# Modulation batches placed directly behind the next group of small matmuls, instead of by a clock of their own

## The chip, the core and the metric

The kernel runs on one core of a Trainium2 chip. The metric is the device time of one execution in microseconds; for the kernel before it is 1811.66 us, the median of three runs (1810.25 to 1814.02). The engines are named as in the profile: PE (TensorE, matmuls), PEld (its weight loads), DVE (VectorE), ACT (ScalarE), POOL (GpSimd) and SP (SyncE, which here issues most DMAs). SP, like every engine, runs its instructions strictly in its own order.

## The reference, cut to what matters

One layer of a hybrid diffusion backbone is computed for 128 context tokens and 256 latent tokens, D = 2048, all in float32. The adaLN modulation is one product of a vector per token kind with a wide matrix:

```python
m = jax.nn.silu(cond) @ w + b          # cond (n, 2048), w (2048, 6 * 2048)
sh1, sc1, g1, sh2, sc2, g2 = jnp.split(m[:, None, :], 6, axis=-1)
hcur = x * (1 + sc1) + sh1             # then h @ w_in: attention, conv module, SSD scan
x = layer_norm(ALPHA * x + g1 * mix)   # mix = concat(three mixers) @ w_out
hcur = x * (1 + sc2) + sh2             # then the ConvFFN, gated by g2
```

Two of its six parts matter here: g1 (the gate of the first residual) and sc2 (the scale ahead of the ConvFFN). They are needed only after w_out, so their products can be done at any time before.

## The kernel before, in words

**The main stream.** Each large float32 product is done as three fp32r products (high parts and low parts of both operands), on PE, back to back, with whole 128x128 weights. They are recorded at L454 to L456 (tokens on the output partitions) and L460 to L462 (channels on the output partitions); this text calls each such instruction a *main*. Weights come from HBM in 512 KB pieces: SP issues the load into one of four `raw` buffers (L216), ACT copies it into a high part (L229), DVE subtracts for the low part (L230).

**The small work.** Between the mains, while the w_in columns of z/dt, v, k and q and the first column group of w_out are computed, PE also does everything that is small and float32: transposes of tokens (L418, L424), cumulative sums of dt (L498 to L503), states and chunk products of the scan (L541, L579, L584, L592, L608), LayerNorm sums (L372, L385), and attention: scores (L698, L701, L703), transposes of the probabilities (L726) and values (L739). They share two PSUM buffers (`at`); a group that needs a third waits until ACT or DVE has copied the first out.

**The modulation batches.** For g1 and sc2, 64 pieces of 512 KB (`wm`) are read. One piece gives four small matmuls with 32 output partitions and 256 columns (L786, each two PE instructions, so a batch of three pieces shows as x24). The pieces come in batches of three, into the three `v` buffers, so the loads of the next batch can be issued only as the matmuls of this one free the buffers. There are 22 batches, the 11th and 22nd of two pieces. After the 11th, `mod2_end(0)` adds the bias (L800, DVE) in a `v` buffer and writes the rows of g1 to HBM (L803, POOL); the third piece of batch 12 takes that buffer. After the 22nd, `mod2_end(1)` turns sc2 (L805, L809, L811).

**What sets the order.** On PE, the order in this stretch is the order in which the program is written out. `_Flow` keeps a planner's clock: `tick(us)` advances it with each group of mains, and a heap holds generators with the time at which each may go on. A generator yields (cost, delay): the cost advances the clock, and after the delay it may place its next group. The generators are `tok_gen`, `dt_gen`, `ssm_gen`, `conv_ln_gen`, `attn_gen`, `sh2_gen` and `mod2_gen(3, 12.0)`, whose 12.0 is the delay between the loads of a batch and its matmuls. `run` is called at most every 1.5 us of that clock. The other engines' queues are ordered by a scheduler that is not changed, from the same program.

Of the kernel before, what the change touches and what calls it, by code (L numbers as in the profile page):

```python
# [47 lines left out]
class _Flow:  # L48
# [2 lines left out]

    def __init__(self, step):
        self.now, self.last, self.n, self.q, self.bg, self.credit, self.step = 0.0, 0.0, 0, [], [], 0.0, step
        self.rate = 0.0

    def add(self, delay, gen):
        self.n += 1
# [2 lines left out]
    def run(self):  # L60
        self.last = self.now
        while self.q and self.q[0][0] <= self.now:
            gen = heappop(self.q)[2]
            said = next(gen, None)
            if said is not None:
                self.now += said[0]
                self.add(said[1], gen)

    def tick(self, us):
        self.now += us  # L70
# [12 lines left out]
    def drain(self):  # L83
        while self.bg:
            self.bg.pop(0)[0]()
        while self.q:
            self.advance()


# [10 lines left out]
def _build(tc, ctx, a):  # L100
# [16 lines left out]
    flow = _Flow(1.5)  # L117
# [232 lines left out]
    def conv31_steps(i):  # L350
        def first():
            do_glu(i)
            cvo[i] = t_t(399)
            V.tensor_scalar(out=cvo[i][:, :399], in0=glu[i][:, 0:399], scalar1=P_("conv_w", 31 * i),
                            scalar2=P_("conv_b", i), op0=ALU.mult, op1=ALU.add)

        def tap(j):
            V.scalar_tensor_tensor(out=cvo[i][:, :399], in0=glu[i][:, j:j + 399], scalar=P_("conv_w", 31 * i + j),
                                   in1=cvo[i][:, :399], op0=ALU.mult, op1=ALU.add)

        return [(first, 1.2)] + [(lambda j=j: tap(j), 0.63) for j in range(1, 31)]
# [46 lines left out]
    def do_conv5(i):  # L408
        o = t_t(386)
        taps(o, xbc_raw[i], lambda j: ("sconv_w", 5 * i + j), 5, P_("sconv_b", i), 386)  # L410
        S.activation(out=o, in_=o, func=AF.Silu)
        xact[i] = o

    def tok_gen():
        for c in range(3):
            ps = at_t()
            for i in range(4):
                PE.transpose(ps[:, 128 * i:128 * i + 128], xact[i][:, OFF[c]:OFF[c] + 128], ident)  # L418
            xtok[c] = m_t()
            S.copy(out=xtok[c], in_=ps)  # L420
            yield 0.5, 1.5
            ps = at_t()
            for i in range(2):
                PE.transpose(ps[:, 128 * i:128 * i + 128], xact[4 + i][:, OFF[c]:OFF[c] + 128], ident)  # L424
            btok[c] = sbt([128, 256], "btok", 3)
            S.copy(out=btok[c], in_=ps[:, :256])
            yield 0.3, 1.5
        ready.add("tok")
# [187 lines left out]
    def ssm_gen():  # L616
        while not {"tok", "dt"} <= ready:
            yield 0.0, 1.0
        yield from state_steps(0, 0)
        yield from state_steps(0, 1)  # L620
        yield from chunk_steps(0)
        load_state()
        yield from state_steps(1, 0)
        yield from state_steps(2, 1)
        yield from chunk_steps(1)
        yield from chunk_steps(2)
        ready.add("ssm")
        ready.update(range(12, 16))
# [147 lines left out]
    def mod2_start(g):  # L776
        gS[g] = gm_t()

    def mod2_load(i):
        g, half, k = i // 32, i // 16 % 2, i % 16  # L780
        return load(a["wm2"][g, half, k], 1024, v_t().rearrange("p a b -> p (a b)"))

    def mod2_piece(i, raw):
        g, half, k = i // 32, i // 16 % 2, i % 16
        for j in range(4):
            PE.matmul(gS[g][32 * j:32 * j + 32, 256 * half:256 * half + 256], cond[:, k, :],  # L786
                      raw[:, 256 * j:256 * j + 256], start=k == 0, stop=k == KC - 1)
# [5 lines left out]
    def mod2_end(g):  # L793
        ps = gS.pop(g)
        vv = v_t()
        sm, bg = vv[:, 0, :], vv[:, 1, :]
        if g == 0:
            pinned(bg, a["bgate"])
            with tc.high_priority(offset=HP):
                V.tensor_tensor(out=sm, in0=ps, in1=bg, op=ALU.add)  # L800
            gd[g] = dr.tile([2, D], F32, tag=f"gd{g}", name=nm("gd"))
            for j in range(4):
                G.dma_start(out=gd[g][:, 512 * j:512 * j + 512], in_=sm[32 * j:32 * j + 2, :])  # L803
            return
        V.tensor_copy(out=sm, in_=ps)  # L805
        yield 0.0, 2.0
        pt = at_t()
        for b in range(4):
            PE.transpose(pt[:, 128 * b:128 * b + 128], sm[:, 128 * b:128 * b + 128], ident)  # L809
        pv = pt.rearrange("p (b j c) -> p j b c", b=4, j=4)[:, :, :, 0:2]  # L810
        V.tensor_tensor(out=s2.rearrange("p (j b) c -> p j b c", j=4), in0=pv,  # L811
                        in1=bc(b2p.rearrange("p (j b) -> p j b", j=4), 3, 2), op=ALU.add)
        yield 0.5, 1.0

    def mod2_gen(most, gap):
        i = 0
        while i < 64:
            n = min(most, 32 - i % 32)
            raws = [mod2_load(j) for j in range(i, i + n)]
            yield 0.0, gap  # L820
            if i % 32 == 0:
                mod2_start(i // 32)
            for j, raw in enumerate(raws):
                mod2_piece(i + j, raw)
            i += n
            yield 0.45 + 0.43 * n, 0.0
            if i % 32 == 0:
                yield from mod2_end((i - 1) // 32)
# [52 lines left out]
    def sh2_gen(gap):  # L881
        while "ssm" not in ready:
            yield 0.0, 1.0
        for _ in range(3):
            sh2_load()
            yield 0.0, gap
        while "stop" not in ready:
            sh2_step()
            yield 0.0, gap
# [103 lines left out]
    with tc.manual_schedule(engines={mybir.EngineType.PE}):  # L993
        for i in range(8):
            do_conv5(i)
        for i in range(4):
            flow.bg += conv31_steps(i)
        flow.rate = 0.45
        flow.add(30.0, tok_gen())
        flow.add(0.0, mod2_gen(3, 12.0))  # L1000
        flow.add(40.0, conv_ln_gen())
        flow.add(30.0, ssm_gen())
        flow.add(50.0, attn_gen())
        flow.add(60.0, sh2_gen(4.0))
        phase_zd()
        flow.add(0.0, dt_gen())
        phase_v()
        flow.rate = 0.7
        for hp in range(8):
            k = qk_tile(0, hp)  # L1010
            qk[hp] = (qk_tile(1, hp), k)
        ps = [mm_t() for _ in range(3)]
        for k in ORDER[:12]:
            cat_split(k)
        wo_group(0, ps, cat_split, lambda last: flow.tick(2.09))
        ready.add("stop")
        flow.drain()
        gb = mix_rows(0)
        for t in range(3):
            mix_evac(t, 0, 0, 512, ps[t], gb)  # L1020
# [333 lines left out]
```

## Time and profile before

| what | value |
|---|---|
| median of three runs | 1811.66 us (1810.25 to 1814.02) |
| the profiled execution's own time | 1812.03 us |
| its span, first to last instruction | 1810.2 us |
| PE busy | 1780.8 us, 98% of the span |
| DVE busy | 1213.4 us, 67% |
| ACT busy | 774.6 us, 43% |
| modulation batches L786, first and last start | 240.4 us, 571.6 us |
| granted TensorE clock, mean | 0.998 |

The table says how long each engine had work. A PE that is busy 98% of the time leaves little room, but "busy" counts the pipelined length of a matmul, so a start-to-start distance is the better measure of what one costs. Idle time of PE is listed with what ended it.

### The profile page before, as it was taken

The page shows a single profiled execution, that of the slowest core. Times are in us where ns is not written, and L with a number is a line of the kernel's source. Part 1 is how long each engine was busy: PE and PEld are TensorE (multiplying, and loading weights), DVE is VectorE, ACT ScalarE, POOL GpSimd, SP SyncE. Part 2 cuts the span into 40 slices and gives each one's busy share as a digit, 9 for nine tenths or more (in the row PEclk, how much of TensorE's full clock was granted, in tenths as well). Part 3 has the DMA queues.
Part 4 walks back from the last instruction along what each step waited for, and adds up shares of the span by engine and source line. Part 5 has one row for each costly group of instructions (what it writes and reads, how often), then busy time and mean ns, then how long its engine had stood idle before and what let it go on. Part 6 is the DMA issues. An engine that isn't in the chain of part 4 may idle for free. (4 is left out here: it accounts for less than half of the span.)

```text
span 1810.2 us, 28844 instructions
## 1 busy us (share of the span) xinstructions
PE 1780.8 (98%) x10794; PEld 1620.9 (90%) x10794; DVE 1213.4 (67%) x2591; ACT 774.6 (43%) x1466; POOL 62.6 (3%) x149
## 2 busy tenths in 40 slices
PE   7999999999999999999999999999999999999998
PEld 6888997888887899999889999989999988999987
DVE  3866899885999566667535667535676544766577
ACT  4222454656764246444433444323444323444434
POOL 0000001110001000000000000000000000000000
PEclk9999999999999999999999999999999999999999
DMA  8999457766999452445444454444544544444454
GB/s 317 310 322 321 148 199 254 241 210 204 356 344 336 138 162 86 142 140 161 130 129 152 151 175 162 135 128 134 175 163 145 158 123 140 163 146 153 121 152 139
DMA packets 113259, 337.75 MB, mean 187 GB/s; under 512 B 13096, under 2 KB 17672, under 8 KB 113120
## 3 DMA queue, kind: packets, MB, share of 16 engines
q1 hardware_dynamic: 105888, 311.65, 52.2%
q0 software_dynamic: 7232, 24.28, 4.5%
q8 instruction: 84, 1.38, 0.3%
q14 instruction: 55, 0.45, 0.1%
HBM read 331.08 MB, written 4.79 MB: 186 GB/s over the span
## 5 line engine op out<-in xcount | busy, mean ns | idle before, releaser
L229 ACT CAST whi<-raw 128x512 fp32r<-128x512 f32 (+1 forms) x755 | 467.5, 620 | 869.1 <-PE mm L461 291.4
L230 DVE TENSOR_TENSOR wlo<-raw,whi 128x512 fp32r<-128x512 f32 (+1 forms) x755 | 519.8, 689 | 428.3 <-ACT whi L229 426.4
L460 PE MATMUL mm<-hl,whi 128*128 128x384 f32 x1245 | 425.2, 342 | 1.4 <-ACT whi L229 1.1
L461 PE MATMUL mm<-hl,whi 128*128 128x384 f32 x1245 | 419.5, 337 | 0.0
L462 PE MATMUL mm<-hl,wlo 128*128 128x384 f32 x1245 | 418.8, 336 | 0.0
L460 PEld LDWEIGHTS mm<-hl,whi 128*128 128x128 f32 x1245 | 233.6, 188 | 12.2 <-issue 5.5
L461 PEld LDWEIGHTS mm<-hl,whi 128*128 128x128 f32 x1245 | 233.8, 188 | 0.6 <-DVE wlo L230 0.2
L462 PEld LDWEIGHTS mm<-hl,wlo 128*128 128x128 f32 x1245 | 233.7, 188 | 0.0
L460 PE MATMUL sc<-hl,whi 128*128 128x384 f32 x659 | 222.8, 338 | 0.0
L461 PE MATMUL sc<-hl,whi 128*128 128x384 f32 x659 | 221.8, 337 | 0.0
L462 PE MATMUL sc<-hl,wlo 128*128 128x384 f32 x659 | 221.7, 336 | 0.0
L460 PEld LDWEIGHTS sc<-hl,whi 128*128 128x128 f32 x659 | 123.6, 188 | 2.9 <-ACT whi L229 1.6
L461 PEld LDWEIGHTS sc<-hl,whi 128*128 128x128 f32 x659 | 123.7, 188 | 0.1
L462 PEld LDWEIGHTS sc<-hl,wlo 128*128 128x128 f32 x659 | 123.7, 188 | 0.0
L843 DVE SCALAR_TENSOR_TENSOR junk<-raw,gb 128x512 bf16<-128x512 f32 x128 | 87.6, 684 | 51.1 <-DMA raw<-wg 50.9
L454 PE MATMUL mm<-whi,hl 128*128 128x512 f32 (+2 forms) x293 | 101.2, 345 | 0.1
L456 PE MATMUL mm<-whi,hl 128*128 128x512 f32 (+2 forms) x293 | 99.4, 339 | 0.0
L455 PE MATMUL mm<-wlo,hl 128*128 128x512 f32 (+2 forms) x293 | 99.3, 339 | 0.0
L456 PE MATMUL mm<-whi,t 128*128 128x512 f32 (+1 forms) x232 | 89.6, 386 | 0.0
L454 PE MATMUL mm<-whi,t 128*128 128x512 f32 (+1 forms) x232 | 89.6, 386 | 0.0
L843 DVE SCALAR_TENSOR_TENSOR junk<-m,m 128x512 bf16<-128x512 f32 x128 | 87.9, 687 | 2.5 <-DMA m<-wsh 0.6
L455 PE MATMUL mm<-wlo,t 128*128 128x512 f32 (+1 forms) x232 | 89.5, 386 | 0.0
(353 smaller groups left out, 2474.8 us busy)
## 6 DMA issues: line engine op xcount, KB each, us to landing
raw<-wu SPq DMA_DIRECT2D x176, 512.0 KB, 3.5
raw<-wd SPq DMA_DIRECT2D x79, 512.0 KB, 3.6
m<-wm SPq DMA_DIRECT2D x128, 256.0 KB, 5.7
v<-wm SPq DMA_DIRECT2D x64, 512.0 KB, 6.4
raw<-wA SPq DMA_DIRECT2D x32, 512.0 KB, 5.4
raw<-wqk SPq DMA_DIRECT2D x32, 512.0 KB, 4.5
m<-wsh SPq DMA_DIRECT2D x64, 256.0 KB, 6.1
raw<-wo SPq DMA_DIRECT2D x32, 512.0 KB, 4.7
```

The source lines that it names most:

```text
L229: S.copy(out=hi[:, :w], in_=rw)
L230: V.tensor_tensor(out=lo[:, :w], in0=rw, in1=hi[:, :w].bitcast(F32), op=ALU.subtract)
L454: PE.matmul(ps[:, :n], A, hi[:, w0:w0 + n], start=k == 0, stop=False)
L455: PE.matmul(ps[:, :n], A, lo[:, w0:w0 + n], start=False, stop=False)
L456: PE.matmul(ps[:, :n], B, hi[:, w0:w0 + n], start=False, stop=k == last)
L460: PE.matmul(ps[:, :T], A, hh[k], start=k == k0, stop=False)
L461: PE.matmul(ps[:, :T], A, hl[k], start=False, stop=False)
L462: PE.matmul(ps[:, :T], B, hh[k], start=False, stop=k == k1)
L843: V.scalar_tensor_tensor(out=j, in0=w, scalar=1.0, in1=cbc[s], op0=ALU.mult, op1=ALU.mult, accum_out=macc[:, 16 * s + kt, kq:kq + 1])
```

## The change

`mod2_gen` yields a delay of None after its loads have been there for the gap, which is now 4.0 instead of 12.0. The planner takes such a generator out of the heap and keeps it in `behind`; as soon as any generator has placed a group with a cost, all generators in `behind` are put at the front of the heap, so that a batch comes directly after that group. `drain` lets those that still wait go on at the end.

```diff
+        self.rate, self.behind = 0.0, []
...
             if said is not None:
                 self.now += said[0]
-                self.add(said[1], gen)
+                if said[1] is None:
+                    self.behind.append(gen)
+                else:
+                    self.add(said[1], gen)
+                if said[0] > 0:
+                    for other in self.behind:
+                        self.add(-1.0, other)
+                    self.behind = []
...
             raws = [mod2_load(j) for j in range(i, i + n)]
             yield 0.0, gap
+            yield 0.0, None
...
-        flow.add(0.0, mod2_gen(3, 12.0))
+        flow.add(0.0, mod2_gen(3, 4.0))
```

The lines added stand above the code, so a line number of the changed kernel is higher by 9 (or 10, below `mod2_gen`): its L795 is L786 here, L735 is L726, L707 is L698, L508 is L499.

**PE, 1926 mains into the main stream, in the attention of a pair of heads.** `gm` is the PSUM of the modulation, `v` a modulation piece; `at`, `p` and `sc` belong to attention. Before, batch 16 stands alone between mains:

```order
L462 MATMUL mm_5483<-hl_80,wlo_5487 128x384
L786 MATMUL gm_4726<-v_5344,cond_63 32x256 x4
L786 MATMUL gm_4726<-v_5346,cond_63 32x256 x4
L786 MATMUL gm_4726<-v_5348,cond_63 32x256 x4
L460 MATMUL mm_5483<-hl_80,whi_5486 128x384
```

At the same place of the main stream now batch 21 stands behind the transposes and scores:

```order
L471 MATMUL mm_5573<-hl_80,wlo_5577 128x384
L735 MATMUL at_5594<-cons_66,p_5481 128x128 x3
L735 MATMUL at_5600<-cons_66,p_5488 128x128 x3
L707 MATMUL sc_5606<-qk_5429,qk_5571 128x128
L707 MATMUL sc_5607<-qk_5429,qk_5571 128x128
L795 MATMUL gm_4536<-v_5516,cond_63 32x256 x4
L795 MATMUL gm_4536<-v_5518,cond_63 32x256 x4
L795 MATMUL gm_4536<-v_5520,cond_63 32x256 x4
L469 MATMUL mm_5573<-hl_80,whi_5576 128x384
```

Over the whole stretch 54 interruptions of the main stream became 42. Before, 8 of the 22 batches stood alone, 6 stood at the head of a group ahead of a full-width matmul, and 3 ended a group of scores; now none stands alone, and 11 follow scores directly.

**SP, where batch 11 has been loaded.** `v<-wm` are modulation pieces, `raw<-wqk` weights of the main stream, `v<-bgate` the bias of g1, `o_k` an output. Before:

```order
L216 DMA raw_4794<-wqk 128x1024
L216 DMA v_4395<-wm 128x1024
L216 DMA v_4397<-wm 128x1024
L171 DMA v_4553<-bgate 128x512
L216 DMA raw_4853<-wqk 128x1024
L216 DMA raw_5010<-wqk 128x1024
L216 DMA v_4561<-wm 128x1024
L216 DMA v_4563<-wm 128x1024
L684 DMA o_k<-qk_4627 128x128
L216 DMA raw_5135<-wqk 128x1024
L216 DMA v_4565<-wm 128x1024
```

Now:

```order
L225 DMA raw_4812<-wqk 128x1024
L225 DMA v_4382<-wm 128x1024
L225 DMA v_4384<-wm 128x1024
L180 DMA v_4428<-bgate 128x512
L225 DMA raw_4923<-wqk 128x1024
L225 DMA v_4436<-wm 128x1024
L225 DMA v_4438<-wm 128x1024
L225 DMA v_4440<-wm 128x1024
L225 DMA raw_5099<-wqk 128x1024
```

The pieces of batch 12 stand together and one weight load closer to those of batch 11; the third (`v_4565`, now `v_4440`) reuses the buffer that held the bias, and its load waits until the rows of g1 have been written out of it.

**DVE, between the two copies of the cumulative sums (`cs<-at`).** PE's L501 waits for the second copy. `vt` is the accumulator of v, `sc` and `mm` PSUM of the main stream. Before:

```order
L499 COPY cs_89<-at_3263 128x3x8
L358 SCALAR_TENSOR_TENSOR t_3231<-g_3225,par_68,t_3231 128x399
L230 TENSOR_TENSOR wlo_3359<-raw_3356,whi_3358 128x512
L667 TENSOR_TENSOR vt_326<-vt_326,sc_3085 128x512
L667 TENSOR_TENSOR vt_327<-vt_327,sc_3086 128x512
L667 TENSOR_TENSOR vt_328<-vt_328,mm_3087 128x512
L230 TENSOR_TENSOR wlo_3363<-raw_3356,whi_3362 128x512
L499 COPY cs_89<-at_3263 128x3x8
```

Now:

```order
L508 COPY cs_89<-at_3245 128x3x8
L367 SCALAR_TENSOR_TENSOR t_3213<-g_3207,par_68,t_3213 128x399
L239 TENSOR_TENSOR wlo_3335<-raw_3332,whi_3334 128x512
L508 COPY cs_89<-at_3245 128x3x8
```

The three additions into `vt` and one low part, which stood between the copies, stand behind the second copy now.

## Rows read from the trace of the kernel before

**Rows 1.** The page: busy time and share of the span by engine, then what the DMAs moved, in 40 slices of 45 us.

```profile
PE 1780.8 (98%) x10794; PEld 1620.9 (90%) x10794; DVE 1213.4 (67%) x2591; ACT 774.6 (43%) x1466; POOL 62.6 (3%) x149
...
GB/s 317 310 322 321 148 199 254 241 210 204 356 344 336 138 162 86 142 140 161 130 129 152 151 175 162 135 128 134 175 163 145 158 123 140 163 146 153 121 152 139
```

**Rows 2.** The waits of PE over the whole execution: the line that waited, for which engine and tile, then us in total, times, longest.

```profile
PE at L726 <- ACT t L742: 3.9, 7, 1.1
...
PE at L726 <- ACT p L716: 1.1, 2, 0.9
PE mm L460 <- ACT whi L229: 1.1, 1, 1.1
PE at L809 <- DVE v L805: 0.6, 1, 0.6
```

**Rows 3.** PE's instructions in order of time around a batch that stands alone between mains (start, length, engine, line, operation, tiles, shape, count).

```profile
523.00 0.34 PE L462 MATMUL mm<-hl,wlo 128*128 128x384 f32 x1
...
523.52 0.34 PE L462 MATMUL mm<-hl,wlo 128*128 128x384 f32 x1
523.79 1.50 PE L786 MATMUL gm<-v,cond 128*32 128x256 f32 x24
525.23 0.44 PE L460 MATMUL mm<-hl,whi 128*128 128x384 f32 x1
525.51 0.34 PE L461 MATMUL mm<-hl,whi 128*128 128x384 f32 x1
```

**Rows 4.** The same view of two groups of transposes and scores, from the last main ahead of each to the second main after it: first with a batch at its head, then without a batch.

```profile
408.67 0.33 PE L462 MATMUL mm<-hl,wlo 128*128 128x384 f32 x1
408.93 1.50 PE L786 MATMUL gm<-v,cond 128*32 128x256 f32 x24
...
412.30 0.34 PE L461 MATMUL mm<-hl,whi 128*128 128x384 f32 x1
...
500.53 0.34 PE L462 MATMUL mm<-hl,wlo 128*128 128x384 f32 x1
...
502.00 0.39 PE L703 MATMUL sc<-ckv,qk 64*128 64x128 f32 x4
502.31 0.44 PE L460 MATMUL mm<-hl,whi 128*128 128x384 f32 x1
502.59 0.34 PE L461 MATMUL mm<-hl,whi 128*128 128x384 f32 x1
```

**Rows 5.** The same view of a batch directly behind scores.

```profile
493.60 0.39 PE L703 MATMUL sc<-ckv,qk 64*128 64x128 f32 x4
493.92 1.50 PE L786 MATMUL gm<-v,cond 128*32 128x256 f32 x24
495.35 0.45 PE L460 MATMUL mm<-hl,whi 128*128 128x384 f32 x1
```

**Rows 6.** The modulation matmuls (length in ns: shortest, median, longest; first and last start in us), then the loads of three batches: first and last issue in us, and below each the time from issue to landing (fastest, middle, slowest of the three); last the page's row over all 64 loads (KB each, median us to landing).

```profile
L786 PE MATMUL gm<-v,cond x512: 379/379/404, 240.4 to 571.6; 128*32 128x256 f32 x171
...
L216 SPq DMA_DIRECT2D v<-wm x3: 328/373/376, 241.1 to 242.0; - x3
...
DMA to landing us min/median/max: 4.7/5.5/6.3
...
L216 SPq DMA_DIRECT2D v<-wm x3: 327/372/382, 289.4 to 290.3; - x3
...
DMA to landing us min/median/max: 3.7/4.5/5.3
...
L216 SPq DMA_DIRECT2D v<-wm x3: 327/382/666, 446.0 to 446.9; - x3
...
DMA to landing us min/median/max: 8.0/8.9/9.7
...
v<-wm SPq DMA_DIRECT2D x64, 512.0 KB, 6.4
```

**Rows 7.** Batch 11 and what hangs on it, in order of time: the batch on PE, the bias on DVE, the write of g1 on POOL, the load of batch 12's third piece on SP with its time to landing.

```profile
395.27 1.07 PE L786 MATMUL gm<-v,cond 128*32 128x256 f32 x16
...
396.65 0.68 DVE L800 TENSOR_TENSOR v<-gm,v 128x512 f32<-128x512 f32 x1
...
397.62 2.03 POOL L803 DMA_DIRECT2D gd<-v  x4 [7.47 <-DVE v L800]
...
404.18 0.33 SPq L216 DMA_DIRECT2D v<-wm  x1
...
DMA to landing us min/median/max: 4.0/4.0/4.0
```

**Rows 8.** DVE and PE ahead of L501, in order of time; in brackets the wait ahead of an instruction and what ended it.

```profile
283.35 1.37 DVE L667 TENSOR_TENSOR vt<-vt,sc 128x512 f32<-128x512 f32 x2
...
285.99 0.17 DVE L499 COPY cs<-at 128x24 f32<-128x24 f32 x1
...
286.22 0.42 PE L501 MATMUL at<-dA,cons 128*128 128x48 f32 x2 [1.53 <-DVE cs L499]
```

**Rows 9.** PE in order of time: five products of the scan between mains.

```profile
323.04 0.34 PE L462 MATMUL mm<-hl,wlo 128*128 128x384 f32 x1
323.21 1.00 PE L584 MATMUL at<-m,m 128*128 128x64 f32 x8
...
324.50 0.34 PE L461 MATMUL mm<-hl,whi 128*128 128x384 f32 x1
```

More of the change, by code (lines that the diff above doesn't have):

```diff
@@ L53, in __init__ @@
         self.now, self.last, self.n, self.q, self.bg, self.credit, self.step = 0.0, 0.0, 0, [], [], 0.0, step
-        self.rate = 0.0
+        self.rate, self.behind = 0.0, []
     def add(self, delay, gen):
@@ L85, in drain @@
             self.bg.pop(0)[0]()
-        while self.q:
+        while self.q or self.behind:
+            while self.behind:
+                self.add(0.0, self.behind.pop())
             self.advance()
```

## The prediction

> **What bounds the kernel now.** I read the page first: PE is busy 98% of the span, DVE 67%, ACT 43% [rows 1], at a mean granted clock of 0.998 of full by the table above. So the end is set by PE's own stream, and a change counts by what it does to start-to-start distances on PE and to the moments when PE stands still. Next I read the list of PE's waits: they are few, and in the stretch of the change nearly all belong to small groups: the two PSUM banks of attention (L726 for L742, 3.9 us in seven waits), the sums of dt (L501, 1.53 [rows 8]), the first probabilities (1.1), the end of the modulation (L809, 0.6); weights of the main stream came late once, 1.1 us [rows 2]. No wait of PE for a modulation piece stands there: with 12 us between loads and matmuls all 64 arrive in time. Then I read the timeline around batches that stand alone, in front of and behind another group, because the change moves batches from the first two kinds to the third. Last came the loads, since the change shortens the time they have.
>
> **Part 1: what a batch costs by its place.** Mains with 384 columns follow each other every (523.52 - 523.00) / 3 = 0.173 us [rows 3]. Alone: from the last main ahead of the batch to the second behind it 525.51 - 523.52 = 1.99, less two such distances 1.64 us [rows 3]. At the head of transposes and scores: 412.30 - 408.67 = 3.63 against 502.59 - 500.53 = 2.06 without a batch, so 1.57 [rows 4]. Directly behind scores: the batch begins 0.32 after the last scores, as a main does without a batch (502.00 to 502.31) [rows 4, 5], and the main then comes 495.35 - 493.92 later, so it adds 1.43. The reason shows in these rows: a batch fills 128x32 of the array, scores 64x128, mains and transposes 128x128; each change of that shape adds about 0.1 us at the boundary (523.52 to 523.79 is 0.27 instead of 0.173), and the first main after a change is followed late. Behind scores one such boundary is shared; behind a full-width group none is, and I count 1.64 there. Before: 8 alone x 1.64, 6 at a head x 1.57, 3 behind scores x 1.43, 5 others at about 1.6: 34.8 us. Now 11 x 1.43 and 11 x 1.64: 33.8. The regrouping is worth **-1.0 us**, not the 12 x 1.6 that 12 interruptions fewer suggest, as the batches' own matmuls stay. Bounds: 0 (all as if alone but for noise) to -2.5 (all 12 vanished boundaries worth the 0.21 of the difference between alone and behind scores).
>
> The Trainium skill (TensorEngine Tiling (Array Packing), Key Properties) says that changing the tiling mode, not merely the tile, drains TensorE. Counted that way the order has 103 changes of shape before and 96 now, which at 0.1 us would give -0.7 instead of -1.0; the rows above agree with the rule, and it speaks against expecting more.
>
> **Part 2: waits of the small groups.** L501 waited 1.53 us because its copy on DVE stands behind the additions into `vt`, which wait for the end of a main group [rows 8]. In the changed order of DVE the copy stands ahead of these additions, and a batch (1.4 us) stands on PE between the two sums, so this wait goes: **-1.5** (between -1.6 and 0). What is late next there is nothing, as nine mains cover the copy. The first probabilities waited about 1 us [rows 2]; four products (0.8 us) now stand behind the first scores besides the batch, so most of it goes. Seven waits of L726 for L742 stay, as the batch comes behind them. New neighbours in the `at` banks cost some: at one place the transposes now follow 2 mains after the main that frees a weight buffer on which ACT's queue, and with it their probabilities, hangs, worth up to 1 us. Together I take **-0.7** (between -2.5 and +2).
>
> **Part 3: supply of the modulation pieces.** The three loads of a batch can be issued only as the matmuls of the previous batch free the three buffers. Before, 22 batches lay between 240.4 and 571.6 [rows 6], 15.8 us apart on average. In the new order I add up mains and groups between batches: batch 15 to 16 is a batch (1.43), one product (0.3), 12 mains x 0.173 = 2.1, transposes and scores 1.6 [rows 4] and five products 1.1 [rows 9], together about 6.6 us from start to start. In the same way: 1 to 2 8.8, 5 to 6 7.2, 8 to 9 9.7, 9 to 10 8.4, 10 to 11 6.6, 17 to 18 7.9, 18 to 19 9.6, 19 to 20 8.4, 20 to 21 9.4; the others 9.7 or more, batch 11 to 12 apart. What is needed: the first load is issued 0.7 after a batch begins (240.4, 241.1), the third 0.9 later, and PE wants the third piece 0.95 after the next batch begins. The set of 241.1 landed its third at 242.0 + 6.3 = 248.3, so a distance of 7.0 was enough; the fastest set (290.3 + 5.3) needs 6.0, the slow one (446.9 + 9.7) 10.4, and the median of 6.4 for one load with 0.8 more for the third needs 7.85 [rows 6]. At 7.85 PE stands 0.65 at batch 6, 0.5 at batch 11 (two pieces), 1.2 at batch 16: 2.3 us. At 6.0 it stands nowhere; at 10.4 ten batches stand, 20 us together. I take a little over the median, **+3.0**, since biases and `wsh` loads share the DMAs and SP now has weight loads directly ahead of some batches: bounds 0 and 20. The weights themselves are covered: four `raw` buffers of 24 mains are 17 us ahead, and a load behind a waiting modulation load on SP is late by less than that; without this cover each would cost PE up to its 4 us.
>
> The Trainium skill (DMA: Bandwidth & Descriptors, Anatomy of one DMA) gives a fit of about 2.0 us plus bytes over 436 GB/s for a DMA, measured on another issuing path. For 1.57 MB in three loads that estimate is 5.6 us, less than even the fastest set took here (295.6 - 289.4 = 6.2), so the trace disagrees; by the page no batch would stand, and this part would be 0, as in the first rival.
>
> **Part 4: batch 12.** Its third piece takes the buffer of the g1 bias. From batch 11's begin to that piece's landing the chain took 404.18 + 4.0 - 395.27 = 12.9 us: batch, bias on DVE, write by POOL, landing of the write, load [rows 7]. All these steps stay. The distance 11 to 12 is now about 9.1 (batch 1.0, 24 mains 4.2, transposes and scores 1.2, products 2.6), so PE wants the piece at 9.1 + 0.95 = 10.05, 0.3 later with a bank's wait: PE stands **+2.6**. Bounds: 0, if waits between the two batches lengthen the distance, and 4, if the bias itself, loaded behind batch 10's pieces, is late. Behind this load on SP stand one weight load and batch 13, both with time to spare (12.8 us from 12 to 13).
>
> **Sum.** -1.0 - 1.5 - 0.7 + 3.0 + 2.6 = +2.4 us on the profiled execution's 1812.03, which is 0.4 above the median shown; on the median 1811.66 + 2.4 = about **1814.0 us**. Two runs of this kernel can be told apart by about 0.2%, 3.6 us, so this is no measurable change, on the slow side.
>
> **Rivals.**
> - *The loads arrive in time.* The stalls of parts 3 and 4 are small because the loads run at the fast set's pace (distance 6.0) and the write of g1 lands sooner when fewer transfers compete. For it: in the stretch before 450 us the DMAs moved 199 to 254 GB/s, against 356 later [rows 1], and the largest gains of part 2 stand in the order of the queues. Against it: the median load took 6.4 and the chain of 12.9 has no DMA rate in it. Then -3.2, with another -1.5 if the banks' waits thin out: 1807.5 us.
> - *Supply decides, on the slower side.* More bytes per time make each set slower than the median, as in the set of 446.0: with a needed distance of 9.2, batches 2, 6, 10, 11, 16, 18 and 20 stand 0.4, 2.0, 0.8, 1.8, 2.5, 1.3 and 0.8: 9.6 in place of 3.0, sum +9.0, 1820.7 us. It decides from a needed distance of about 8.3 on, where the sum passes 3.6. For it: modulation and weights together ask for some 300 GB/s where 1.57 MB come each 9 us (175) and 0.52 MB of weights each 24 mains, 4.2 us (125), close to the most that a slice shows (356). Against it: most sets before 440 us stayed near the first one.
> - *A new wait takes L501's place*: the waits of part 2 come out at +2 instead of -2.2; the sum is then +6.6, 1818.2 us, and it counts with the slower side.
>
> **How the numbers follow.** Forecast (within 0.2% of before, 1808.0 to 1815.3): 0.41. Loads in time, faster by over 0.2%: 0.21. Slower by over 0.2%: 0.38, of which 0.28 for supply and 0.10 for new waits. The forecast's own range is 1809 to 1818. The range for 8 in 10 runs from the first rival's time, 1807.5, to the second's, 1821.
>
> **What would show it.** Right: PE waits at the batches' line with a `v<-wm` load as the cause, most of it in batches 6, 11, 12 and 16, 5 to 6 us together; the wait of L501 gone; a batch behind scores adding 1.43; 42 interruptions. Part 3 is wrong if the list of waits has under 1 us or over 8 us for these loads, part 4 if batch 12 begins its third piece without a wait, part 2 if the waits for `at` banks grow by over 2 us. The forecast as a whole falls if weights (L229) or the last column groups of w_out begin to wait, which none of its terms contains.

## The result, and the profile after

The changed kernel takes 1827.51 us, median of six runs (1823.03 to 1831.16); the kernel before, run beside it, 1812.24 (1810.25 to 1814.02). The ratio is 1.0083, 95% interval 1.0073 to 1.0094: slower by 15 us, where 1814.0 had been forecast with a range up to 1821. The profiled execution took 1827.43 us; PE is as busy as ever, as in [rows 1], and only longer:

```profile
span 1825.7 us, 28869 instructions
PE 1787.2 (98%) x10794; PEld 1625.0 (89%) x10794; DVE 1213.7 (66%) x2591; ACT 774.9 (42%) x1466; POOL 61.3 (3%) x149
```

The waits of PE in the stretch of the small work (215 to 620 us), which answer to [rows 2]; columns are total us, how often, the longest:

```profile
PE gm L795 <- DMA v<-wm: 6.3, 5, 2.2
PE at L735 <- ACT p L725: 4.2, 1, 4.2
PE at L735 <- DVE m L558: 3.1, 1, 3.1
PE at L735 <- ACT t L751: 2.3, 7, 0.6
PE at L818 <- DVE v L814: 1.3, 1, 1.3
PE at L507 <- DVE cs L508: 0.5, 1, 0.5
```

L501's wait of [rows 8] is gone (L510 is not in the list), and the waits of `at` banks for L751 fell from 3.9 to 2.3. Against that stand 6.3 us for modulation pieces (none before), 4.2 for the probabilities `p` (1.1 before) and 3.1 for L558.

From the start of main 901 to that of main 2501, read off the trace, the kernel before needs 413.6 us and this one 427.3. These 13.7 us are nearly all of the 15.4 between the two spans; the parts ahead and behind differ by 1.1 and 0.6. Because several experiments below keep PE's order, the time between the same two groups can be compared in all of them. The stretches are named by the start of their first and last group in the changed kernel, in us. Each row is one execution; that of experiment 9 was the slowest of its four, that of experiment 10 the fastest of its five.

| kernel | 324–336: batch 6 | 345–368: L558, batch 8 | 368–433: batches 9 to 14 | 483–514: batches 20 to 22 | 514–546: `p` |
|---|---|---|---|---|---|
| changed kernel | 12.3 | 23.1 | 64.9 | 31.8 | 31.4 |
| experiment 1 | 11.4 | 20.6 | 58.9 | 27.7 | 31.2 |
| experiment 2 | 12.2 | 23.8 | 60.8 | 27.7 | 31.2 |
| experiment 3 | 12.6 | 21.4 | 65.2 | 35.0 | 27.1 |
| experiment 5 | 11.4 | 22.4 | 59.3 | 27.7 | 27.1 |
| experiment 6 | 12.7 | 23.2 | 60.7 | 27.7 | 27.1 |
| experiment 9 | 16.6 | 23.7 | 59.9 | 32.4 | 31.4 |
| experiment 10 | 12.5 | 21.5 | 58.6 | 33.6 | 27.1 |
| experiment 16 | 12.7 | 23.0 | 63.6 | 32.3 | 27.9 |

Against the lowest of each column the changed kernel loses 0.9, 2.5, 6.3, 4.1 and 4.3 us, 18 in all. Without them it would need some 409 us, four less than the kernel before. No single run reached that, and the kernel before has waits of its own, so the four us are not the regrouping alone; that is priced below.

**The largest single wait** is in the timeline (start, length, engine, line). The transposes of 546 us wait for `p`, whose scaling (L725) stands on ACT behind 16 casts of the concatenation (L254) and three weight casts:

```profile
538.36 0.69 ACT L254 CAST hl<-t 128x128 fp32r<-128x128 f32 x3
538.95 0.61 ACT L238 CAST whi<-raw 128x512 fp32r<-128x512 f32 x1
539.47 2.56 ACT L254 CAST hl<-t 128x128 fp32r<-128x128 f32 x7
541.94 0.62 ACT L238 CAST whi<-raw 128x512 fp32r<-128x512 f32 x1
542.46 0.71 ACT L254 CAST hl<-t 128x256 fp32r<-128x256 f32 x2
543.07 0.62 ACT L238 CAST whi<-raw 128x512 fp32r<-128x512 f32 x1
543.59 1.75 ACT L254 CAST hl<-t 128x384 fp32r<-128x384 f32 x4
545.24 1.12 ACT L725 ACTIVATE p<-p,sm 128x384 f32<-128x384 f32 x2
545.91 1.05 PE L735 MATMUL at<-cons,p 128*128 128x128 f32 x6 [4.17 <-ACT p L725]
...
549.26 0.52 PE L471 MATMUL mm<-hl,wlo 128*128 128x384 f32 x1
549.58 0.52 PE L469 MATMUL mm<-hl,whi 128*128 128x384 f32 x1
```

The last two rows show a second cost: after the stand, mains come 0.32 us apart instead of 0.174. The windows view (columns: length, busy time of PE, PEld, DVE, ACT, POOL with counts, granted clock, DMA share, GB/s) has the granted clock at half there, 1.2 instead of 2.4 GHz, and at full again behind it. The last three rows are the other stretches at half clock between 215 and 620 us; the kernel before has none there:

```profile
538.00:545.90 7.90, 3.75 (x22) 3.42 (x20) 7.77 (x23) 7.90 (x23) 0.00 (x0) 1.00 0.54 156
546.90:550.30 3.40, 3.40 (x15) 3.01 (x15) 3.30 (x9) 0.55 (x2) 0.00 (x0) 0.51 0.34 117
550.40:553.80 3.40, 3.40 (x18) 2.99 (x17) 3.40 (x13) 2.83 (x8) 1.08 (x2) 1.00 0.92 295
359.20:362.60 3.40, 3.40 (x27) 1.78 (x31) 1.77 (x5) 2.52 (x9) 0.00 (x0) 0.50 0.09 34
389.90:393.30 3.40, 3.40 (x17) 2.62 (x13) 1.23 (x2) 0.96 (x2) 2.04 (x4) 0.50 0.86 306
403.60:407.00 3.40, 3.23 (x28) 2.58 (x24) 3.29 (x5) 0.67 (x2) 0.87 (x2) 0.50 0.90 298
```

**What half clock costs.** In experiment 15 the same instructions of PE ran at full clock in all four places. The table has the time from the start of the first to the start of the last of them, less PE's waits among them, in us:

| first and last start in the changed kernel | changed kernel | experiment 15 |
|---|---|---|
| 355.75 to 363.26 (half clock from 359) | 4.43 | 2.86 |
| 389.47 to 393.81 (from 390) | 4.34 | 2.85 |
| 403.25 to 407.67 (from 404) | 4.25 | 2.80 |
| 546.58 to 550.82 (from 547) | 4.23 | 2.67 |

The four differences add up to 6.1 us. PE's waits between main 901 and main 2501 add up to 17.9 us, against 9.4 before, so 8.5 more. Clock and waits together make 14.6 us; as the whole difference is 13.7, the regrouping itself is left with −0.9. The executions agree that the clock matters: of the six, the fastest (1823.03 us) had a mean granted clock of 0.997, the slowest (1831.16 us) one of 0.990.

**The chain of g1.** The bias, issued by SP behind batch 11's pieces at 381.8 us, landed 8.2 us later, at 390.0. The matmuls of batch 11, which had stood for their own pieces, ended at 390.1, so bias and matmuls released DVE's addition within 0.1 us of each other. Then POOL wrote the rows, SP issued the third piece of batch 12 at 396.3 us, and PE stood until it had landed. First the bias, then that third piece, then the steps:

```profile
L180 SPq DMA_DIRECT2D v<-bgate x1: 383/383/383, 381.8 to 381.8; - x1
DMA to landing us min/median/max: 8.2/8.2/8.2
```

```profile
L225 SPq DMA_DIRECT2D v<-wm x1: 328/328/328, 396.3 to 396.3; - x1
...
DMA to landing us min/median/max: 6.3/6.3/6.3
```

```profile
387.37 0.64 PE L795 MATMUL gm<-v,cond 128*32 128x256 f32 x8 [0.45 <-DMA v<-wm]
389.45 0.67 PE L795 MATMUL gm<-v,cond 128*32 128x256 f32 x8 [1.44 <-DMA v<-wm]
...
390.17 0.69 DVE L809 TENSOR_TENSOR v<-gm,v 128x512 f32<-128x512 f32 x1 [1.96 <-PE gm L795]
391.15 2.04 POOL L812 DMA_DIRECT2D gd<-v  x4 [7.96 <-DVE v L809]
...
399.78 1.07 PE L795 MATMUL gm<-v,cond 128*32 128x256 f32 x16
402.68 0.64 PE L795 MATMUL gm<-v,cond 128*32 128x256 f32 x8 [1.82 <-DMA v<-wm]
```

### The profile page after: what moved, and what is told of

The parts are those of the page before. It is cut to its first block, busy times and chain, and to the rows that moved or that the text cites. A ratio compares the mean times of both kernels' runs of the same rounds, so it can differ in the third digit from the quotient of the medians.

```text
span 1825.7 us, 28869 instructions
## 1 busy us (share of the span) xinstructions
PE 1787.2 (98%) x10794; PEld 1625.0 (89%) x10794; DVE 1213.7 (66%) x2591; ACT 774.9 (42%) x1466; POOL 61.3 (3%) x149
## 5 line engine op out<-in xcount | busy, mean ns | idle before, releaser
L469 PEld LDWEIGHTS mm<-hl,whi 128*128 128x128 f32 x1245 | 234.1, 188 | 13.7 <-issue 7.9
L853 DVE SCALAR_TENSOR_TENSOR junk<-m,m 128x512 bf16<-128x512 f32 x128 | 87.9, 687 | 12.2 <-DMA m<-wsh 10.2
```

The source lines that it names most:

```text
L469: PE.matmul(ps[:, :T], A, hh[k], start=k == k0, stop=False)
L853: V.scalar_tensor_tensor(out=j, in0=w, scalar=1.0, in1=cbc[s], op0=ALU.mult, op1=ALU.mult, accum_out=macc[:, 16 * s + kt, kq:kq + 1])
```

## The experiments

Each starts from the changed kernel unless the diff is of the kernel before. PF stands for the edit of experiment 3, G1 for that of experiment 13. Experiments 1, 2, 3, 13 and 16 carry the account of the cause; most of the others look for an order without the new waits, and find none.

**1. No supply.**

```diff
+        sm = bg = m_t()
...
+            if i == 0:
+                first = [mod2_load(j) for j in range(3)]
+            raws = first[:n]
```

> The changed kernel with its three first modulation pieces kept and used for all 64 (the other 61 loads are left out, so g1 and sc2 come out of wrong weights), and the bias of g1 in an m buffer; PE's order is that of the changed kernel. Theory S (supply: the loads come too late for batches that stand closer, and PE standing for them also takes the clock down): of the 15.4 us of the two profiled executions, the stands at batches 6, 8, 11, 12 and 21 go (1.0 + 1.5 + 2.2 + 3.9 + 2.7 = 11 us with the half-clock stretches at them), so 1815 to 1818 us, ratio to before 1.002 to 1.004, and no wait of L795 for v. Theory N (new waits of the small groups for ACT and DVE in the changed order): most stays, the waits for p at L735 (4.2) and for m of L558 (3.1) stand as they were, and 1821 to 1825 us, ratio 1.005 to 1.007.

Measured: 1814.31 us, ratio to before 1.0016 (1.0006 to 1.0025). Theory S, a little beyond it: 13.2 us of the loss hang on the loads, with what they cost other transfers beside them, and the chain of g1. But the wait for `p` stayed (3.9), and so did 2.1 for L558; N explains what is left.

**2. The bias of g1 (and sc2's copy) in another buffer.** The first line of the diff above alone.

> The changed kernel with the bias and the sum of g1 (and sc2's copy) in an m buffer instead of a v buffer, so that batch 12's third piece no longer waits for the write of g1. Theory S with the chain of g1 as its largest part: the 3.9 us of batch 12 fall to under 1, 1823.5 to 1825 us. If the loads themselves are the limit there, batch 12 still waits for its pieces and the time falls by under 1.5 us. Theory N: no change (under 1 us), or a new wait for an m buffer.

1818.41 us, ratio 1.0038 (1.0025 to 1.0051), 9.1 less: more than twice what was expected. Batch 12 no longer stands, but the stretch of batches 20 to 22 also lost 4.1 us. A side effect offers itself as the reason: with sc2's copy in an `m` buffer, no `wsh` load is issued between 465.0 and 495.1 us, a time in which the changed kernel issues nine. Experiments 13 and 16 take the two apart.

**3. Probabilities first.**

```diff
         for e in range(2):
+          with tc.high_priority(offset=HP):
             nmx, sm = s_t(1), s_t(1)
```

(and the lines that follow it, to the scaling.)

> The changed kernel with the steps from scores to probabilities (max, exp, reciprocal, scaling) put ahead on ACT and DVE, so that they don't stand behind the casts of the concatenation. PE's order is the same. Theory N: the wait of L735 for p at 546 us (4.2 us, with its half-clock stretch after it 5.4 us) goes, so 1821.5 to 1823 us, and no half-clock stretch at 547. Theory S: this wait is one disturbance among others and its removal gives under 2 us, or comes back as another wait at the same place.

1823.91 us, ratio 1.0065 (1.0050 to 1.0080), 3.6 less, just outside theory N's range. The scaling now stands ahead of the casts, PE does not wait, and the clock stays up at 547:

```profile
540.20 0.61 ACT L726 ACTIVATE p<-p,sm 128x384 f32<-128x384 f32 x1
540.72 0.89 ACT L254 CAST hl<-t 128x128 fp32r<-128x128 f32 x4
```

This stretch fell by 4.3, but part of it came back in another: sc2's copy was later, with a wait of its own.

```profile
PE at L819 <- DVE v L815: 3.9, 1, 3.9
```

**4. Placement with the old 12 us.** `mod2_gen(3, 12.0)`.

> The changed kernel with the old 12 us between loads and matmuls, so the batches still stand behind other groups, but as far apart as before. Theory S: PE stands for v nowhere (under 0.5 us) and the time is that of before less the regrouping, 1809 to 1814 us, ratio 0.998 to 1.001. Theory N: the small groups stand at new places again, waits for ACT and DVE of 3 us and more stay, 1816 to 1822 us, with no wait for v.

1830.69 us, ratio 1.0106 (1.0090 to 1.0123). A miss on both sides, as the kernel was badly chosen: every batch now waits 12 us and then for a group, some 20 us from batch to batch, so that 14 pieces were left over. They run one by one in w_out, the first after a stand:

```profile
PE gm L795 <- DMA v<-wm: 8.8, 2, 8.2
```

**5. No supply, small groups first.** Experiment 1 with PF and high priority on the product of L589 and the copy of L814. (The expectation says L558 for L589: the line that was edited is the chunk product, and L558, the state's addition, was left as it was.)

> The first kernel (three pieces kept, the other 61 loads left out, so g1 and sc2 come out of wrong weights; the bias of g1 in an m buffer) with the small groups' steps put ahead on ACT and DVE: the probabilities, the product of L558 and the copy of L814. What is left is the regrouping alone. Theory (the 2.8 us by which the first kernel is still above before are waits of L735 for ACT and DVE, 3.9 and 2.1 us with the half-clock stretch behind them, less the gains of the regrouping): 1807 to 1809 us, ratio 0.9975 to 0.9985, L735's waits for p and m under 1 us and no half-clock stretch between 215 and 620 us. Rival (the waits move to other instructions as they did when the probabilities alone were put ahead, or the regrouping itself costs): 1811 to 1815 us.

1810.88 us, ratio 0.9995 (0.9986 to 1.0005); the wait for `p` is gone, 2.3 for L558 stayed. Between the two figures; of the theory's signs, the wait for `p` and its half clock went and L558's wait did not. Without any supply and without the wait for `p` the changed order is level with the kernel before.

**6. The same with all pieces loaded.**

> The changed kernel with the bias of g1 in an m buffer and the same three steps put ahead, all pieces loaded. Theory (supply without the chain of g1 is worth the 4.1 us between the second and the first kernel): 4 us above the kernel before this one, 1811 to 1813 us, the same as before. Rival (waits move): 1814 to 1817 us.

1814.74 us, ratio 1.0015 (1.0006 to 1.0025). The time is in the rival's range, but the step from experiment 5 is the theory's: supply in this kernel, which has no `wsh` load beside batch 21 either, costs 3.9 us. It is the fastest kernel of this study that loads all pieces and has the new placement, and it is not faster than before.

**7. The same edits on the kernel before.**

> The kernel before with the same edits (bias in an m buffer, the three steps put ahead). Theory: what these edits cure is made by the changed order, so here they find little: the waits of L726 for p (1.1) and for m (1.4), 1 to 2 us, 1809.5 to 1811 us. Rival: the edits help any order by 4 us and more, and then they say nothing on the change.

1827.04 us, ratio 1.0092 (1.0077 to 1.0107): a miss, by the edit itself. From main 901 to main 2501 it takes 410.9 us, 2.7 less than before. But sc2's copy in an `m` buffer came so late here that the `wsh` products were pushed back into the LayerNorm at 670 us, where DVE alternates between them (L845) and the rows that PE waits for (L1049). The whole time therefore can't tell the two expectations apart; 2.7 us in the stretch lie between them:

```profile
684.33 0.54 DVE L1049 TENSOR_SCALAR vt<-vt,sm,sm 128x512 f32<-128x512 f32 x1
684.78 0.68 DVE L845 SCALAR_TENSOR_TENSOR junk<-m,m 128x512 bf16<-128x512 f32 x1
```

**8. Five us instead of four**, with the buffer of experiment 2: `mod2_gen(3, 5.0)`.

> The changed kernel with the bias of g1 in an m buffer and 5 us instead of 4 between loads and matmuls: the batches between 1620 and 2211 mains lie some 60 mains apart instead of 30. Theory (the closeness of the batches costs the 4.1 us that are left of the supply): waits of L795 for v under 1 us, 1814 to 1817 us. Rival (the supply that is left is not a matter of the spacing, or the groups' order that changes with it brings waits of its own): 1818 us or more.

1830.45 us, ratio 1.0103 (1.0085 to 1.0121), spoiled by the same side effect. Its stretch is clean: 413.0 us from main 901 to main 2501, and no wait for `v` in the list. Half of its batches lie 45 mains or more behind the last one, against 30 in the changed kernel. That fits closeness as what makes the loads late, but the groups behind which the batches stand changed with it.

**9. L558 in program order**, with the bias of g1 alone in an `m` buffer.

```diff
+        if g == 0:
+            sm = bg = m_t()
+        else:
+            sm = v_t()[:, 0, :]
...
-            V.tensor_tensor(out=o, in0=o, in1=ps, op=ALU.add)
+            tc.keep_in_program_order(V.tensor_tensor(out=o, in0=o, in1=ps, op=ALU.add))
```

(L573's product likewise.)

> The changed kernel with the bias of g1 in an m buffer (sc2's copy stays in a v buffer) and the steps L558 and L573 kept in program order on DVE, so that L558, on which L735 waits for a bank, no longer stands behind an L573 that waits for a transfer of POOL. Theory (this wait is one of two of the changed order that cost the small groups more than the regrouping gives): the group with L550, L735 and batch 8 falls from 9.1 us (second kernel) to about 4.5, the time to 1813 to 1815.5 us. Rival (the decays are late instead and L593 or L735 wait for them): 1817 to 1819 us.

1824.87 us, ratio 1.0073 (1.0059 to 1.0086), above both figures; the wait is 3.6, where the changed kernel had 3.1. Its timeline points to POOL and not to an L573 on DVE as what holds L558 up: the masks wait for their transfer, ACT's exponentials for the masks, the weight cast behind them on ACT, the low part of the weight on DVE, and L558 behind that:

```profile
358.13 0.96 POOL L569 TENSOR_SCALAR_AFFINE_SELECT m<-m 128x512 f32<-128x512 f32 x1 [2.91 <-DMA m<-csd]
...
359.13 0.40 ACT L572 ACTIVATE m<-m,ncs 128x128 f32<-128x128 f32 x1 [1.50 <-POOL m L569]
...
361.20 0.60 ACT L238 CAST whi<-raw 128x512 fp32r<-128x512 f32 x1
361.84 0.69 DVE L239 TENSOR_TENSOR wlo<-raw,whi 128x512 fp32r<-128x512 f32 x1 [1.07 <-ACT whi L238]
362.45 0.68 DVE L558 TENSOR_TENSOR m<-m,at 128x512 f32<-128x512 f32 x1
363.27 0.52 PE L735 MATMUL at<-cons,p 128*128 128x128 f32 x3 [3.59 <-DVE m L558]
```

**10. Experiment 9 with PF and L814's copy first.**

> The kernel before this one with the probabilities and the copy of L814 put ahead as well: all waits that were named are treated, all pieces are loaded. Theory: 1809 to 1812 us, the same as before within what can be told, because the regrouping (1 us), L501's wait (1.5) and the treated waits stand against some 4 us of supply. Rival: waits move again, 1813 us or more.

1819.09 us, ratio 1.0043 (1.0030 to 1.0057): the rival. The stretch of `p` is mended (27.1), that of batches 20 to 22 is not (33.6).

**11. The same priorities and order on the kernel before.**

> The kernel before with the same edits on the probabilities, L805, L549 and L564, its modulation unchanged. Theory: its waits for p (1.1) and m (1.4) go, 1808.5 to 1810.5 us, so that even the mended change gains nothing over the mended kernel before. Rival: no change or slower, 1811.5 us or more.

1813.90 us, ratio 1.0011 (1.0002 to 1.0020): no gain. The waits for `p` and `m` went; one of 2.0 us for the copy of `qk` came instead.

**12. Batch 6 later**, experiment 10 with 6 us for that batch.

> The kernel before the last with 6 instead of 4 us of delay for batch 6 alone, which shifts all batches from 6 on to other groups (6 lies 63 mains behind 5 instead of 24, and 12 lies 30 mains behind 11 instead of 24). Theory (what is left of supply is set by the closest pairs, 5 to 6 and 10 to 11): waits for v under 1 us in all, 1808 to 1811 us. Rival (another order has other waits of the same size): 1812 us or more.

1822.45 us, ratio 1.0057 (1.0044 to 1.0071). Half right: the waits for `v` fell to 1.3 us, but the groups met other waits, as the rival had it:

```profile
PE at L550 <- ACT pt L738: 4.3, 1, 4.3
PE at L736 <- DVE m L558: 3.8, 1, 3.8
PE at L822 <- DVE sm L725: 2.6, 1, 2.6
```

**13. The bias of g1 alone** (the first four lines of the diff of experiment 9).

> The changed kernel with only the bias and sum of g1 in an m buffer (sc2's copy stays in a v buffer, no other edit). Theory (the chain of g1 alone is worth what stands between the groups at 368 and 433 us, 64.9 us in the changed kernel and 59.9 in the ninth): that stretch falls by about 5 us, and the stretch from 483 to 514 us stays at 32 us, since the wsh loads run in it as in the changed kernel: 1821 to 1824 us. Rival (the second kernel's 9 us were all from the buffer of g1): 1817 to 1819 us.

1823.00 us, ratio 1.0057 (1.0041 to 1.0072), 4.5 less than the changed kernel: the theory's time. The profiled execution was the slowest of its four (1828.71) and bears the theory out in part. Batch 12 does not stand and batch 21 still does, for 2.5 us, with `wsh` loads beside it; but the stretch of batches 9 to 14 is 64.5 us long, with 6.8 us at half clock in it from 391.7 on. Experiments 1, 2, 5, 6, 9 and 10, which lack the chain too, have 58.6 to 60.8 us there.

**14. The wsh loads after the batches.** `sh2_gen` waits for the last batch.

> The changed kernel with the wsh loads begun only after the last modulation batch, at shorter steps (2.5 instead of 4.0). Theory (batches 21 and 22 stand because wsh and modulation loads share the time of the DMAs; in the second kernel, where no wsh load fell there, they did not stand): the stretch from 483 to 514 us falls from 31.8 to 27.7 us, the others stay, 1822 to 1824.5 us. Rival (those batches stand because of sc2's copy or of the pieces' own spacing): the stretch stays at 31 us or more, 1826 us or more.

1827.80 us, ratio 1.0084 (1.0070 to 1.0098). It tested nothing: the scheduler pulled the loads, which have high priority, ahead again.

**15. G1, PF, L814's copy first, order of experiment 9 and the waiting `sh2_gen`.**

> The changed kernel with all that the runs point to: bias of g1 in an m buffer, probabilities and L814's copy put ahead, L558 and L573 in program order, wsh loads after the batches. Theory (every stretch falls to the lowest that a run has shown for it, but for batches 6, 8 and 11 with their own loads): between main 900 and main 2500 about 411 us against 413.6 of the kernel before, 1808 to 1811.5 us, ratio 0.998 to 1.000. Rival (a wait comes back elsewhere, as in four of the kernels so far): 1813 us or more.

1819.79 us, ratio 1.0037 (1.0024 to 1.0050): the rival; 3.8 us of wait for sc2's copy.

**16. The wsh loads held behind batch 21.**

```diff
-        with tc.high_priority(offset=HP):
-            nc.sync.dma_start(out=w, in_=a["wsh2"][kq, kt // 2, :, 512 * (kt % 2):512 * (kt % 2) + 512])
+        pinned(w, a["wsh2"][kq, kt // 2, :, 512 * (kt % 2):512 * (kt % 2) + 512])
```

(The modulation loads likewise, and `sh2_gen` starts 10 us of planner's time after the last batch and goes in steps of 1 us instead of 4.)

> The changed kernel with the wsh loads really behind the loads of batch 21 on SP (both kinds keep their program order there; in the run before this one the scheduler had pulled the wsh loads ahead again, so that it tested nothing). Theory (batch 21 stands because of the wsh transfers beside it): batch 21's third piece lands within 8 us of its issue, the group at 493 us costs 2.7 instead of 5.3 to 6.3 us, the stretch from 483 to 514 us falls from 31.8 to between 27.7 and 29.5 (the copy of L814 stays late), the time by 3 us, 1822 to 1825. Rival (the stand is of the batches' own spacing, or of the bias and row transfers of POOL): the group stays at 5 us or more.

1839.26 us, ratio 1.0159 (1.0144 to 1.0174), far above the expectation, yet its question is answered. Batch 21's three loads by tile, in the changed kernel and then here (us to landing: least, median, most):

```profile
who waited for it (us, times):
  PEld gm L795: 3.1, 2
  PE gm L795: 2.2, 1
...
DMA to landing us min/median/max: 6.7/8.7/11.1
```

```profile
who waited for it (us, times):
busy tenths in 40 slices 0000000000200000000000000000000000000000
DMA to landing us min/median/max: 3.9/5.3/7.9
```

Its group costs 2.7 us instead of 5.3 and PE does not stand. The stretch from 483 us stayed at 32.3 all the same, since PE stood 2.8 us in it ahead of the transposes of sc2 (L820). Most of the time went elsewhere: PE waited 10.8 us in three waits for the probabilities, with the `wsh` work crowded behind the batches.

**17. The same with G1, PF and L814's copy first.**

> The same with the bias of g1 in an m buffer and the probabilities and L814's copy put ahead. Theory: 4.5 us for the chain of g1 and 4.5 for the probabilities off the run above, 1812 to 1816 us; the order is then at best level with the kernel before (1812). Rival (a new wait, as in other mended kernels): 1817 us or more.

1828.71 us, ratio 1.0105 (1.0088 to 1.0122): the rival; DVE and ACT are late for w_out's first mains (3.6 and 1.4 us) and for sc2's copy (2.9), and 3.5 us of waits for pieces are left.

**18. Five us, G1 and PF.**

> The eighth kernel (5 us instead of 4) with only the bias of g1 in an m buffer, so that sc2's copy no longer pushes the wsh products into the LayerNorm at 670 us, and with the probabilities put ahead. Theory (with some 60 mains between batches the supply is in time, the g1 chain is cured, and the regrouping is worth a few us): no wait for v, main 901 to main 2501 in 410 to 413 us as in the eighth kernel (413.0) or a little below, the rest as before: 1808.5 to 1812 us, ratio 0.9985 to 1.0005. Rival (the order brings another wait): 1814 us or more.

1818.05 us, ratio 1.0032 (1.0020 to 1.0045): the rival. The waits of its small groups, with `v` no longer the first of them:

```profile
PE at L736 <- DVE m L558: 3.6, 1, 3.6
...
PE mm L463 <- ACT qk L689: 2.2, 1, 2.2
...
PE gm L796 <- DMA v<-wm: 1.8, 2, 1.2
```

No kernel of this study beats the kernel before by what can be told.

## Why the prediction was wrong, term by term

The medians divide the loss. Experiment 1 against before is +2.8: Parts 1 and 2. Experiment 2 against experiment 1 is 4.1 and experiment 13 against experiment 2 is 4.6, together 8.7: Part 3. The changed kernel against experiment 13 is 4.5: Part 4. The sum is 16.0; 0.75 of it is the kernel before itself, which had 1811.49 beside experiments 1 to 4 and 1812.24 beside the changed kernel. By the intervals each of the last three steps is uncertain by some 3 to 4 us. The trace of the one profiled execution divides its 13.7 us in another way: regrouping −0.9; waits of the small groups 2.1 and half clock behind two of them 3.1; waits for pieces of batches 6, 11 and 21 4.5 and half clock behind one of them 1.5; batch 12 1.8 and half clock behind it 1.5. By both, Parts 2 and 3 failed by the most; Part 1, which only the trace has by itself, held.

- **Part 1, −1.0, and L501's wait, −1.5: right.** 42 interruptions stand in the trace and L501's wait is gone. A batch behind scores that does not stand adds the 1.43 us that were counted (experiment 16: batch 21 from 493.15, the next main at 494.58), and the trace leaves −0.9 for the regrouping.
- **Part 2, other waits, −0.7: wrong, Parts 1 and 2 by 6.0 together.** The place was named: transposes two mains behind the main that frees a weight buffer, "worth up to 1 us". It cost 4.2 in one wait and 4.3 in its stretch, where half clock followed. I asked only on which main ACT's queue hung and not how much stood in that queue: 16 casts of the concatenation, placed there by w_out's beginning. The wait for L558 grew from 1.4 to 3.1, by a chain over POOL, ACT and DVE that I hadn't looked at.
- **Part 3, +3.0: measured 8.7 by the medians, 6.0 in the trace.** The mechanism was right, the size and the places were not. One needed distance, 7.85, for all batches was the mistaken step. Batch 16, for which I counted 1.2, did not stand (its loads took 3.7, 4.5 and 5.3 us); batch 6 stood 0.5 (0.65 counted), batch 11 1.9 (0.5 counted), and batch 21, which neither the sum nor the rival named, 2.2, since three `wsh` loads were issued right ahead of its loads and more beside them (11.1 us for the third; 7.9 without them in experiment 16). What a load takes at a place depends on what is issued there, and the order of SP that I had shows it. The Trainium skill's fit (DMA: Bandwidth & Descriptors, Anatomy of one DMA), 5.6 us as an estimate for three loads, agrees with the best set here (6.2, batch 16: 5.3 and 0.9 of issue) far better than with batch 21's.
- **Part 4, +2.6 with an upper bound of 4: measured 4.5 by the medians; in the trace a stand of 1.8 and 1.5 of half clock behind it.** The mechanism was right. The chain from batch 11's begin (387.4) to the landing (402.6) took 15.2 us instead of 12.9, and the distance from batch 11 to 12 12.4 instead of 9.1, as batch 11 stood itself and half clock followed. That the bias alone was late, for which the bound was set, is not shown: it landed as batch 11's matmuls ended. What follows a stand, half clock, was in no bound.
- **The clock stood in no term, and cost 6.1 us.** Four stretches of 3.4 us at half clock, from 359, 390, 404 and 547 us, each came behind a stand of PE of 1.4 to 4.2 us; before, there was none between 215 and 620 us. The prediction had read a mean granted clock of 0.998 and took full clock for the changed order too, although it counted on new stands. In experiment 3, with the stand of 546 us gone, the last of them was gone too. The Trainium skill (TensorE: Matmul & The Clock Gate, Loop structure matters more than you think) gives as its bad case a loop with a long wait for a transfer ahead of every matmul, in which TensorE goes to the lower clock. The trace shows the fall for single stands in a dense stream, and for a wait for ACT (4.2 us at 546) or DVE (3.1 at 359) as well.
- **The rivals.** "Supply decides" put Part 3 at 9.6 (measured 8.7), "a new wait takes L501's place" put the small groups at +2 (Parts 1 and 2 came out at +2.8 instead of +1.0). Both came true at once. I had given each its chance as if it came alone, and ended the range at the worse of the two; with both, the same terms give −1.0 + 2.0 + 9.6 + 2.6 = +13.2, or 1825 us. (The first rival's time doesn't follow from its own terms: −3.2 and −1.5 on 1811.66 give 1807.0, not 1807.5; nothing hangs on it.)

What stays open: which part of the wait for L558 comes of the change. No edit removed it. With the changed placement and 4 or 5 us it lay between 2.1 and 3.8 us; in experiment 4, with 12 us, it was 1.5, about as before. That `wsh` loads also slow batches other than 21 was not tried. No experiment changed the clock alone; its price is read off the trace.

## What to carry to other kernels

When a change shifts a group against the other engines' work, count what stands in the queue ahead of the thing it waits for, not only the event on which that queue hangs. Price a load by what is issued beside it at its place, not by the median of all. A new stand of PE can cost more than its own length, as half clock may follow it. And rivals that have different causes can come true together: the range needs their sum.

## What was not expected of the hardware

Short stands of PE were followed by half clock: batch 11 stood 0.45 and 1.44 us for its two pieces, batch 12 1.82 us for its third, and from 389.9 and 403.6 us on the granted clock was 0.50 for 3.4 us each. Not each stand was followed so: behind the 2.16 us of batch 21, at 497.3 us, the clock stayed at full, and in experiment 15 behind 3.8 us for sc2's copy. Loads of the same size, issued by the same queue in sets of three, took from 3.7 to 11.1 us to land within 46 us of the same execution.
